# Token dispatch scaling on one core: first load cut into 16 and 112 partitions, weight loads moved behind it in the ScalarE queue

## The chip, the core and the metric

The kernel runs on one core of one Trainium2 chip. The metric is device time in microseconds (us), the median of several executions; lower is better.

## What is computed

```python
batch, seq, hidden, n_experts, k = 16, 1024, 512, 8, 2
# x: (16, 1024, 512) float32, expert_weights: (16, 1024, 2) float32
x_expanded = x[:, :, np.newaxis, :].repeat(k, axis=2)
out = x_expanded * expert_weights[..., np.newaxis]    # (16, 1024, 2, 512) float32
```

Every token, a row of 512 floats, is written out twice, each time multiplied by one of its two weights. The indices of the experts are not used. The kernel reads 33.6 MB of x and 0.13 MB of weights and writes 67.1 MB. There is one multiplication for each output element, so nearly all of the work is moving data.

## The kernel before

The 16384 tokens are dealt in eight groups of 2048. In a group each of the 128 partitions holds 16 consecutive tokens, that is 16 x 512 floats or 32 KB in one contiguous row (`rows`, lines 47 to 50).

Three pools hold the tiles. `w_tile` is one tile of 128 x 256 floats for all the weights. `x_pool` has two buffers of 32 KB per partition, each for one whole group. `o_pool` has four buffers of 32 KB per partition, and each of them takes the two products of eight tokens, half a group.

The work is issued from three engines:

- **SyncE queue.** First the eight weight loads (line 55), one for each group: 128 partitions x 32 floats, so 128 runs of 128 bytes, 16 KB in all. Then the sixteen stores (line 91), 4 MB each, one for each filled `o_tile`.
- **ScalarE queue.** The eight loads of x (line 70), 4 MB each: 128 partitions x 8192 floats. ScalarE computes nothing.
- **VectorE.** For every token and each of its two weights one `tensor_scalar` multiply (line 83) of 128 x 512 floats, 256 in all, 32 for each group and 16 for each store.

The order follows from the tile framework, which puts semaphore waits where a tile is written, read or used again. A load of x waits until VectorE is done with the group that lay in its buffer. A multiply that begins a new `o_tile` waits for the store that last used this buffer, four stores earlier. A store waits for its sixteen multiplies.

One more rule of order matters here. [...] In the kernel before, the first x load has semaphore 0 and the weight loads of groups 0 to 6 have 1 to 7 in the order of the program's text. The eighth weight load takes number 0 again, so it waits for the first x load. The second x load takes number 1 again, so it waits for the weight load of group 0. The later transfers wait for ones that ended long before, or for ones whose end they need anyway.

Of the kernel before, what the change touches and what calls it, by code (L numbers as in the profile page):

```python
# [1 line left out]

# [4 lines left out]


@with_exitstack
def kernel(  # L10
    ctx: ExitStack,
    tc: tile.TileContext,
    x: bass.AP,
    expert_indices: bass.AP,
    expert_weights: bass.AP,
    out: bass.AP,
):
    nc = tc.nc

    batch, seq, hidden = x.shape  # L20
    k = expert_weights.shape[-1]
    P = nc.NUM_PARTITIONS
    ntok = batch * seq
    assert ntok % P == 0
    A_TOTAL = ntok // P

    f32 = mybir.dt.float32
    row = k * hidden
    TX = 16
    TO = 8  # L30

    groups = [[[16]], [[16]], [[16]], [[16]], [[16]], [[16]], [[16]], [[16]]]
    assert sum(sum(sum(t) for t in g) for g in groups) == A_TOTAL

    xf = x.rearrange("b s h -> (b s) h")
    of = out.rearrange("b s k h -> (b s) (k h)")
    wf = expert_weights.rearrange("b s k -> (b s) k")

    w_pool = ctx.enter_context(tc.tile_pool(name="w_pool", bufs=1))
    x_pool = ctx.enter_context(tc.tile_pool(name="x_pool", bufs=2))
    o_pool = ctx.enter_context(tc.tile_pool(name="o_pool", bufs=4))

    w_tile = w_pool.tile([P, A_TOTAL * k], f32)

    def rows(of_all, done, T):
        return of_all[done * P : (done + T) * P, :].rearrange(
            "(p a) n -> p (a n)", a=T
        )  # L50

    done = 0
    for group in groups:
        T = sum(sum(t) for t in group)
        nc.sync.dma_start(
            out=w_tile[:, done * k : (done + T) * k], in_=rows(wf, done, T)
        )
        done += T

    done = 0  # L60
    for group in groups:
        T = sum(sum(t) for t in group)
        xr = rows(xf, done, T)
        outr = rows(of, done, T)
        a0 = 0
        for pieces in group:
            x_tile = x_pool.tile([P, TX * hidden], f32)
            at = 0
            for n in pieces:
                nc.scalar.dma_start(  # L70
                    out=x_tile[:, at * hidden : (at + n) * hidden],
                    in_=xr[:, (a0 + at) * hidden : (a0 + at + n) * hidden],
                )
                at += n
            ends = [sum(pieces[: i + 1]) for i in range(len(pieces))]
            first = 0
            for t in range(at):
                if t % TO == 0:
                    o_tile = o_pool.tile([P, TO * row], f32)
                for kk in range(k):  # L80
                    c = (done + a0 + t) * k + kk
                    o = t % TO * row + kk * hidden
                    nc.vector.tensor_scalar(  # L83
                        out=o_tile[:, o : o + hidden],
                        in0=x_tile[:, t * hidden : (t + 1) * hidden],
                        scalar1=w_tile[:, c : c + 1],
                        scalar2=None,
                        op0=mybir.AluOpType.mult,
                    )
                if t + 1 in ends or (t + 1) % TO == 0:  # L90
                    nc.sync.dma_start(
                        out=outr[:, (a0 + first) * row : (a0 + t + 1) * row],
                        in_=o_tile[:, first % TO * row : (t % TO + 1) * row],
                    )
                    first = t + 1
            a0 += at
        done += T


# [1 line left out]
_INS = ['x', 'expert_indices', 'expert_weights']  # L101
_OUTS = [((16, 1024, 2, 512), 'float32')]


# [23 lines left out]
```

## Time and profile before

| | |
|---|---|
| median of 3 runs | 240.84 us (240.41 to 241.1) |
| span of the profiled execution | 239.6 us |
| VectorE busy | 102.5 us (43%), 256 multiplies, mean 480 ns |
| bytes moved by DMA | 100.81 MB, mean 421 GB/s |
| share of 16 DMA engines: weights and stores (q1) | 65.3% |
| share of 16 DMA engines: loads of x (q10) | 33.0% |

The profile is that of one execution. Its times count from the start of the span. DVE is VectorE; ACTq and SPq are the instruction queues of ScalarE and SyncE, from which transfers are issued. The view of 40 slices gives for each slice of 6.0 us the busy share in tenths. The rows of DMA issues give the transfer, the queue, the count, the size of one transfer and the median time from issue to landing. A row of the chain of waits gives the start, the length and what was being waited for. A window row gives the stretch, its length, the busy time of the engines that work, the granted clock, the DMA busy share and the GB/s that were moved. Behind the views lie the trace's packet records: each transfer is cut into packets, and for each packet there are its start, its length, its queue and its size, but not the engine that moved it. A load of x is 128 packets of 32,768 bytes, a weight load 128 packets of 128 bytes.

### The profile page before, as it was taken

Reading aid. Unit: us, or ns where it says so; the run is one execution under the profiler, and the core shown is the slowest. Engines: PE = TensorE matmul, PEld = TensorE weight load, DVE = VectorE, ACT = ScalarE, POOL = GpSimd, SP = SyncE. Lnnn points to the kernel's source line nnn. Section 1 sums busy time; section 2 is a strip of 40 time slices with the busy share of each in tenths; the row PEclk is TensorE's granted clock in tenths of the full one; section 3 lists DMA queues with packets and bytes.
Section 4 is the critical chain, followed back from the end, with each engine's and each line's share of the span. In section 5 each row is a group of like instructions: output and inputs, shape, how many; then the busy total and the mean of one; then the engine's idle time right before and its main releaser. Section 6 shows DMA issues by size and latency. Waiting matters only on the chain.

```text
span 239.6 us, 369 instructions
## 1 busy us (share of the span) xinstructions
DVE 102.5 (43%) x256; POOL 0.2 (0%) x4
## 2 busy tenths in 40 slices
DVE  0089994067701905591064900739008485400000
POOL 0000000000000000000000000000000000000000
DMA  7999999999999999999999999999999999999994
GB/s 265 439 439 367 439 432 438 438 438 438 438 427 432 438 421 432 438 427 438 416 432 421 438 438 421 434 432 438 427 438 432 438 421 427 438 427 432 432 432 197
DMA packets 4610, 100.81 MB, mean 421 GB/s; under 512 B 1536, under 2 KB 1536, under 8 KB 1536
## 3 DMA queue, kind: packets, MB, share of 16 engines
q1 hardware_dynamic: 3456, 67.24, 65.3%
q10 hardware_dynamic: 1152, 33.55, 33.0%
q14 instruction: 2, 0.02, 0.0%
HBM read 33.69 MB, written 67.11 MB: 421 GB/s over the span
## 4 chain that ended last, share of the span: by engine, by line
DMA 62%; DVE 18%; another core or an unknown queue 5%; issue 0%; DVEq 0%
DMA out_dram<-o_tile 56%; DVE o_tile L83 18%; DMA x_tile<-in_x_dram 5%; DVEq L123 0%; DVEq L83 0%
## 5 line engine op out<-in xcount | busy, mean ns | idle before, releaser
L83 DVE TENSOR_SCALAR o_tile<-x_tile,w_tile 128x512 f32<-128x512 f32 x256 | 102.5, 480 | 104.1 <-DMA out_dram<-o_tile 76.4
L112 POOL MEMSET const-bfloat16-1.0<- 128x1 bf16 x1 | 0.1, 103 | 0.0
L112 POOL MEMSET const-uint8-127<- 128x1 uint8 x1 | 0.1, 103 | 0.0
L112 POOL MEMSET const-float32-1.0<- 128x1 f32 x1 | 0.1, 100 | 0.0
L112 POOL MEMSET const-float32-0.0<- 128x1 f32 x1 | 0.1, 99 | 0.2 <-issue 0.2
## 6 DMA issues: line engine op xcount, KB each, us to landing
out_dram<-o_tile SPq DMA_DIRECT2D x16, 4096.0 KB, 45.4
x_tile<-in_x_dram ACTq DMA_DIRECT2D x8, 4096.0 KB, 24.2
w_tile<-in_expert_weights_dram SPq DMA_DIRECT2D x8, 16.0 KB, 20.5
```

The costliest lines, as they stand in the source:

```text
L83: nc.vector.tensor_scalar(out=o_tile[:, o : o + hidden], in0=x_tile[:, t * hidden : (t + 1) * hidden], scalar1=w_tile[:, c : c + 1], scala ...
L112: nc = _bacc.Bacc("TRN2", target_bir_lowering=False, num_devices=1)
```

## The change

The first load of x becomes two loads, one of the partitions 0 to 15 and one of the partitions 16 to 127. All eight weight loads leave the SyncE queue and are issued on the ScalarE queue, right after these two. Then comes the second x load. It is meant to get the first bytes moving with a small transfer, and to keep the weights out of the way of the first load and of the first stores, which have the SyncE queue to themselves.

```diff
-    done = 0
     for group in groups:
-        T = sum(sum(t) for t in group)
-        nc.sync.dma_start(
-            out=w_tile[:, done * k : (done + T) * k], in_=rows(wf, done, T)
-        )
-        done += T
+        weights.append((sum(n for _, n in weights), sum(group)))
+    cuts = [0, 16, 128]
...
+    def load(i):
...
+        x_tile = x_pool.tile([P, TX * hidden], f32)
+        cols = rows(xf, done, T)[:, a0 * hidden : (a0 + n) * hidden]
+        for lo, hi in zip(cuts, cuts[1:]) if i == 0 else [(0, P)]:
+            nc.scalar.dma_start(out=x_tile[lo:hi, : n * hidden], in_=cols[lo:hi, :])
+        loaded.append(x_tile)
+        if i == 0:
+            for at, m in weights:
+                nc.scalar.dma_start(
+                    out=w_tile[:, at * k : (at + m) * k], in_=rows(wf, at, m)
+                )
+    for i in range(2):
+        load(i)
     for i, (done, T, a0, n) in enumerate(tiles):
+        x_tile = loaded[i]
...
-                nc.scalar.dma_start(
-                    out=x_tile[:, at * hidden : (at + n) * hidden],
-                    in_=xr[:, (a0 + at) * hidden : (a0 + at + n) * hidden],
-                )
...
+        load(i + 2)
```

The rest of the diff rewrites the loops and leaves the instructions alike: the same 256 multiplies in the same order on VectorE, the same sixteen stores on SyncE, and the same seven later loads of x. The ScalarE queue of the built program now has seventeen transfers where it had eight, and the semaphores fall differently. With their waits, the first of them are:

```
x_tile<-in_x_dram 16x8192                    semaphore 0
x_tile<-in_x_dram 112x8192                   semaphore 1
w_tile<-in_expert_weights_dram 128x32 x6     semaphores 2 to 7
w_tile<-in_expert_weights_dram 128x32        waits for semaphore 0
w_tile<-in_expert_weights_dram 128x32        waits for semaphore 1
x_tile<-in_x_dram 128x8192                   waits for semaphore 2
```

More of the change, by code (lines that the diff above doesn't have):

```diff
@@ L30 @@
     TO = 8
-    groups = [[[16]], [[16]], [[16]], [[16]], [[16]], [[16]], [[16]], [[16]]]
-    assert sum(sum(sum(t) for t in g) for g in groups) == A_TOTAL
+    groups = [[16], [16], [16], [16], [16], [16], [16], [16]]
+    assert sum(sum(g) for g in groups) == A_TOTAL
     xf = x.rearrange("b s h -> (b s) h")
@@ L50, in rows @@
         )
+    weights = []
+    for group in groups:
+        weights.append((sum(n for _, n in weights), sum(group)))
+    cuts = [0, 16, 128]
+    tiles = []
     done = 0
     for group in groups:
-        T = sum(sum(t) for t in group)
-        nc.sync.dma_start(
-            out=w_tile[:, done * k : (done + T) * k], in_=rows(wf, done, T)
-        )
-        done += T
-    done = 0
-    for group in groups:
-        T = sum(sum(t) for t in group)
-        xr = rows(xf, done, T)
-        outr = rows(of, done, T)
[L65 to L70, printed above, removed]
-                    out=x_tile[:, at * hidden : (at + n) * hidden],
-                    in_=xr[:, (a0 + at) * hidden : (a0 + at + n) * hidden],
-                )
[L74 to L88, printed above, removed]
-                    )
[L90 to L96, printed above, removed]
-        done += T
@@ new lines @@
+        T = sum(group)
+        a0 = 0
+        for n in group:
+            tiles.append((done, T, a0, n))
+            a0 += n
+        done += T
+    loaded = []
+    def load(i):
+        if i >= len(tiles):
+            return
+        done, T, a0, n = tiles[i]
+        x_tile = x_pool.tile([P, TX * hidden], f32)
[8 more added lines that the diff above has]
+                )
@@ new lines @@
+    for i in range(2):
+        load(i)
+    for i, (done, T, a0, n) in enumerate(tiles):
+        x_tile = loaded[i]
+        outr = rows(of, done, T)
+        for t in range(n):
+            if t % TO == 0:
+                o_tile = o_pool.tile([P, TO * row], f32)
+            for kk in range(k):
+                c = (done + a0 + t) * k + kk
+                o = t % TO * row + kk * hidden
+                nc.vector.tensor_scalar(
+                    out=o_tile[:, o : o + hidden],
+                    in0=x_tile[:, t * hidden : (t + 1) * hidden],
+                    scalar1=w_tile[:, c : c + 1],
+                    scalar2=None,
+                    op0=mybir.AluOpType.mult,
+                )
+            if (t + 1) % TO == 0:
+                nc.sync.dma_start(
+                    out=outr[:, (a0 + t + 1 - TO) * row : (a0 + t + 1) * row],
+                    in_=o_tile,
+                )
+        load(i + 2)
```

## Prediction, made before the run

> **What bounds the kernel now.** I read the slices first, then windows cut where the slices dip, then the chain of waits and the waits of the SyncE queue, and last the packet records. The page's slices:
>
> ```profile
> DVE  0089994067701905591064900739008485400000
> DMA  7999999999999999999999999999999999999994
> GB/s 265 439 439 367 439 432 438 438 438 438 438 427 432 438 421 432 438 427 438 416 432 421 438 438 421 434 432 438 427 438 432 438 421 427 438 427 432 432 432 197
> ```
>
> The DMA engines are full from the second slice to the last but one, VectorE is mostly waiting. Windows put numbers on the dips:
>
> ```profile
> 0.00:2.10 2.10, 0.00 (x0) 0.20 (x4) 1.00 0.48 128
> 2.10:4.20 2.10, 0.00 (x0) 0.00 (x0) 1.00 0.91 361
> 4.20:12.50 8.30, 0.00 (x0) 0.00 (x0) 1.00 0.97 416
> 12.50:21.00 8.50, 7.88 (x20) 0.00 (x0) 1.00 1.03 433
> 21.00:24.00 3.00, 3.00 (x9) 0.00 (x0) 1.00 0.89 293
> 24.00:146.00 122.00, 59.52 (x149) 0.00 (x0) 1.00 1.01 434
> 146.00:150.00 4.00, 0.00 (x0) 0.00 (x0) 1.00 0.97 377
> 150.00:236.00 86.00, 32.13 (x80) 0.00 (x0) 1.00 1.00 433
> ```
>
> At 434 GB/s the 100.81 MB take 232.3 us, so only 7.3 us of the 239.6 are not transfer at full rate: the start, a dip at 21 to 24 us, one at 146 us, the tail. The end moves by what the change adds to or takes from the time in which DMA engines stand idle or run slowly. The chain of waits begins with the part that the change touches:
>
> ```profile
> 0.73 12.37 DMA x_tile<-in_x_dram
> 13.09 0.03 issue
> 13.12 8.06 DVE o_tile L83 x21
> ```
>
> VectorE starts when the first load has landed at 13.09. The DMA engines go on without a break at that point, because the second load was issued long before:
>
> ```profile
> 8.24 0.33 ACTq L70 DMA_DIRECT2D x_tile<-in_x_dram  x1
> SPq L55 <- DMA x_tile<-in_x_dram: 8.6, 1, 8.6
> ```
>
> The first line (timeline) is the second x load: it had waited only for the weights of group 0, landed at 8.22. The second (waits of SyncE) is the eighth weight load, which waited for the whole first load. Nothing but stores stood behind it.
>
> The packet records give the unit of the sums. A packet of 32,768 bytes takes 1.213 us (27.0 GB/s; sixteen at once 432) and begins 1.218 us after the one before it. The engines begin their first packets at 1.85 to 2.85 us, mean 2.26, which is 1.53 after the issue at 0.73. The first packets end at 3.97 on average, 0.49 later than 1.213 us would. The first load's last packets end at 12.30 to 12.76, and its landing follows 0.33 later. The second load's packets follow at once; the first store's begin at 23.12 on average. Of the 1024 weight packets 720 run at 22 to 24 us: they alternate with x packets until these run out, then drain, in front of the first store. That is the dip at 21 us.
>
> [...] seven weight loads were issued by 4.4 us, and until the x packets ran out about one weight packet got through for each x packet. [...] The trace before has only 128-partition transfers. [...] no run here shows 16.
>
> **The change part by part.**
>
> *The second x load is issued later.* In the ScalarE queue it now stands behind the last weight load, which waits for the piece of 112 partitions. So nothing more is loaded until the whole first group has landed; call that time L. Queued behind the waiting weight load are all further x loads. The first store can't fill the hole: it needs sixteen multiplies, which begin at L and take 6.45 us (13.12 to the store's issue at 19.57). From L: one weight issue (0.33 to 0.38 us, the last one before took 0.33), then the x issue, then 1.53 us to the mean first packet: 1.9 us. If first packets again end 0.49 late: 2.4. Before, the second load's packets followed without a gap, so this is new idle time of all engines.
>
> *Weights leave the SyncE queue.* The 1024 packets now follow the first load in the same ring and drain in this hole, and the first store finds nothing before it. What that takes away is the dip: in before the first store's packets begin at 23.12 where sixteen x packets in a row end 16 x 1.218 after 2.75 (the first packets' end less one packet), at 22.24: 0.9 us gained. VectorE now also waits for the weights of group 0[...]. I cost it at nothing: while VectorE runs late, the second load keeps the engines busy for 9.7 us, and the first store comes 6.5 us after L.
>
> In one expression: before, the engines had moved 16 x packets each and began on the first store at 23.12, which is as if the second load had begun at 23.12 - 8 x 1.218 = 13.38. After, it begins at L + 1.9 to 2.4. The change is L + 1.9 (2.4) - 13.38. From there on both are full to the end with the same bytes: at L + 12.8 VectorE has freed the buffer for the third load and the second store is issued, while the second load and first store together keep the engines busy past L + 21.
>
> *The first load in two pieces.* If only the engines limit it, L is 13.1, or up to 0.4 less where sixteen descriptors and no weights in the way get the first packets started faster. Lower bound: L = 12.7. [...] With first packets at about 2.05 and the 0.33 of landing, L is 17.0 to 18.2. [...]
>
> *The loops.* Same multiplies and stores, same seven later loads: nothing.
>
> [...] 17.0 + 1.9 - 13.38 = 5.5 to 18.2 + 2.4 - 13.38 = 7.2, middle 6.4: 240.84 + 6.4 = 247.2 us.
>
> **The rivals.**
> - *Only the wait costs.* [...] L = 12.7 to 13.1, the change +1.2 to +2.1: about 242.4 us. For it: the engines' own rate is 27.0 GB/s, and the trace can't tell an engine's limit from a port's.
> - *Faster.* The start improves (0.5 late first packets, 0.4 of spread), the 0.9 us dip goes, and the new hole sets all engines off together, so the tail, where the last store's engines land between 236.4 and 238.8 us, shrinks by about 1 us; the dip at 146 us (57 GB/s short for 4 us, 0.5 us) may go too. The hole is 1.9: 1.9 - 0.9 - 0.9 - 1 - 0.5 = -1.4 with everything lucky, two thirds of it -0.9: about 239.9 us. Against it: the hole is certain from the waits, while tail and late dip have no tie to the first load.
> - *No change.* The same gains cancel the hole: 240.8.
> - *Worse dealing.* If the 112 partitions are dealt in rounds of sixteen neighbours, [...] about 271 us.
>
> **How the numbers follow.** Ports and wait 0.60 (247.2); wait alone 0.20 (242.4); faster 0.12 (239.9); no change 0.03 and worse dealing 0.05. Faster by over 0.3% (below 240.1): 0.12 with the lucky edge of the rest, 0.13. Within 0.3%: 0.07, which takes in the low edge of the wait alone. Slower: 0.80. The range runs from 241.6, leaving out the faster cases and the low edge of the wait alone, to 249.0, which takes in 248.0 and leaves the worse dealing out.
>
> **What would show it.** The second x load issued within 0.5 us after the first group's landing, and a window of about 2 us of almost no traffic there: the wait. [...] VectorE's start at 17 to 18.5 us: the ports; a start near 13 us refutes them. No dip where the first store begins: the weights. Full rate afterwards. I am wrong if the second load is issued before the first has landed, or if the tail's or the late dip's shape moves the end by more than the start does.

## The result, and the profile after

The changed kernel takes 254.0 us (median of 4 runs, 252.88 to 255.11) where the kernel before, run beside it, takes 240.68 us. The ratio is 1.055, with a 95% interval of 1.050 to 1.060. The direction was forecast, the size was not: 247.2 us with a range up to 249.0. The profiled execution of the changed kernel has a span of 251.1 us, 11.5 more than the 239.6 before; it is the fastest of its four runs, 1.1 us below their median, while the profiled execution before (241.35 us) lies 0.7 above its own. That is why the spans differ by 11.5 and the medians by 13.3. Where this text sums up a trace, it compares these two spans.

The 40 slices of the page after (6.3 us each):

```profile
DVE  0004969905463090459109090184503684700000
DMA  9995999999999999999999999999999999999994
GB/s 167 240 251 115 418 418 419 418 418 444 470 418 423 418 433 470 428 418 423 418 459 454 418 418 418 444 471 418 418 423 423 475 418 433 418 423 449 449 428 183
```

Nearly all of the loss is in the first four slices. DMA reads 9 in the first three of them, while the GB/s of the second and third, 240 and 251, are little more than half of the 439 that they were. This is the line to remember: the DMA engines are not idle, each packet takes longer, 3.58 us in the mean for the piece of 16 partitions and 1.8 to 2.7 in the seven steps of the piece of 112, where it was 1.213. Only the fourth slice, with a 5, shows idle engines. The slices after it count packets by their start, so 418 and 470 alternate; windows give the rate (stretch, length, busy time, clock, DMA share, GB/s; a share above 1 comes from packets that begin in a window and end after it):

```profile
1.70:5.50 3.80, 0.00 (x0) 0.00 (x0) 1.00 1.15 172
5.50:20.50 15.00, 0.00 (x0) 0.00 (x0) 1.00 0.97 237
20.50:23.60 3.10, 1.13 (x3) 0.00 (x0) 1.00 0.26 35
23.60:25.80 2.20, 2.20 (x7) 0.00 (x0) 1.00 1.18 373
25.80:30.00 4.20, 4.20 (x12) 0.00 (x0) 1.00 0.99 429
30.00:35.00 5.00, 5.00 (x14) 0.00 (x0) 1.00 1.01 374
35.00:132.00 97.00, 45.46 (x114) 0.00 (x0) 1.00 1.01 435
132.00:246.00 114.00, 44.60 (x112) 0.00 (x0) 1.00 1.00 432
```

The first line is mostly the piece of 16 partitions, the second the piece of 112, the third the hole, the sixth the dip where the first store begins. From 35 us on the rate is that of before. The chain of waits in order of time (start, length, what), from the piece of 112 partitions to the second x load:

```profile
1.13 21.04 DMA x_tile<-in_x_dram
22.16 0.02 issue
22.18 0.34 ACTq L80
22.52 0.04 issue
22.56 15.36 DMA x_tile<-in_x_dram
```

The piece of 112 partitions lands at 22.16, where the whole first load had landed at 13.09. The last weight load (L80) is issued 0.02 us later, and the second x load behind it at 22.56; before, that one went out at 8.24. So the load that began the chain before is followed here by a second one that could not overlap it. VectorE starts 0.3 us after the landing, when the first weights are there:

```profile
DVE o_tile L95 <- DMA w_tile<-in_expert_weights_dram: 22.5, 1, 22.5
```

The packet records of both traces give the account, in means over the sixteen engines (the records don't name them: sixteen packets run at a time, each beginning where one ends):

| | before, us | after, us | difference |
|---|---|---|---|
| end of the first load's last packets | 12.51 | 20.47 | +7.96 |
| from there to the second load's first packets | 0.02 | 3.36 | +3.34 |
| these first packets, beyond 1.213 | 0.00 | 0.70 | +0.70 |
| the last x packets before the first store, beyond 1.213 | 0.38 | 0.73 | +0.35 |
| from them to the store's first packets | 0.47 | 0.00 | -0.47 |
| sum | | | +11.9 |

The spans differ by 11.5. The first row is the split. The next two are the wait; about 0.8 us of the second comes in with the split, because the engines then end further apart (19.91 to 21.11 us, before 12.30 to 12.76) and the landing follows later (1.05 us after the last end, before 0.33); with the wait alone this row is 2.60. The last two are the dip where the first store begins: before, some 700 weight packets run there and leave a gap of 0.47 us; after, no weights are left (1020 of the 1024 packets begin at 19 to 23.6 us, mostly in the hole) and nothing stands before the store, but the x packets just ahead of it are lengthened more.

### The profile page after: what moved, and what is told of

It is laid out like the page before. It is cut to its first block, busy times and chain, and to the rows that moved or that the text cites. A ratio compares the mean times of both kernels' runs of the same rounds, so it can differ in the third digit from the quotient of the medians.

```text
span 251.1 us, 370 instructions
## 1 busy us (share of the span) xinstructions
DVE 102.6 (41%) x256; POOL 0.2 (0%) x4
## 4 chain that ended last, share of the span: by engine, by line
DMA 69%; DVE 12%; another core or an unknown queue 5%; ACTq 0%; DVEq 0%; issue 0%
DMA out_dram<-o_tile 54%; DMA x_tile<-in_x_dram 14%; DVE o_tile L95 12%; DVEq L132 0%; ACTq L76 0%; ACTq L80 0%; DVEq L95 0%
```

## The experiments

The first theory: two costs that add up, one of the split and one of the wait. Four kernels make a square: split or not, second load behind all weights or not. The changed kernel is the corner with both.

**The wait alone.**

```diff
-    cuts = [0, 16, 128]
+    cuts = [0, 128]
```

> The changed kernel with the first load whole again: all weight loads stay on the ScalarE queue ahead of the second x load. Theory (two costs that add up: the split makes the first load about 8 us longer, and the second load waits behind the last weight load): the first load lands at about 13 us, the second is issued right after, the engines stand idle for about 3.4 us and the first packets after that are 0.7 us late, so 240.7 + 4 = about 244.7 us. Rival (the split makes all of it, and the hole behind the first load is filled or made up later): 240.7 to 241.5 us. Rival (the wait makes most of it): 250 us or more.

Measured: 244.59 us, ratio 1.016 (1.009 to 1.022), span 243.3, as the theory had it; both rivals fall. Windows of this kernel:

```profile
1.70:12.50 10.80, 0.00 (x0) 0.00 (x0) 1.00 0.99 391
12.50:14.70 2.20, 1.16 (x3) 0.00 (x0) 1.00 0.34 49
14.70:16.60 1.90, 1.90 (x6) 0.00 (x0) 1.00 0.97 276
22.00:26.50 4.50, 4.29 (x11) 0.00 (x0) 1.00 0.94 350
```

The first load runs at its old speed and lands at 13.26; then there are 2.2 us with next to no traffic, and a slow start. The wait costs 3.7 of span by itself. The fourth line is the dip at the first store: it is there although all weights went through in the hole. By the packet records it is made of x packets lengthened by 0.81 us, with no gap behind them.

**The split alone.** The second load goes ahead of the other weights, so that it waits for nothing.

```diff
-        if i == 0:
-            for at, m in weights:
+        if i < 2:
+            for at, m in weights[:1] if i == 0 else weights[1:]:
```

> The changed kernel with the second x load moved ahead of the weight loads of groups 1 to 7, right behind the weights of group 0, so that it waits for nothing; the first load is still cut into 16 and 112 partitions. Theory of two costs: only the split remains, the first load's last packets end at about 20.5 us instead of 12.5, the second load's follow at once: 240.7 + 8 = about 248.7 us. Rival (the split costs only because it is followed by the wait): 242 us or less. Rival (weights draining in the first seconds of the store queue made the dip of the kernel before): about 0.9 us less than the theory, 247.8 us.

Measured: 249.2 us, ratio 1.035 (1.028 to 1.041), span 247.3. Its windows:

```profile
1.70:5.50 3.80, 0.00 (x0) 0.00 (x0) 1.00 1.32 198
5.50:20.50 15.00, 0.00 (x0) 0.00 (x0) 1.00 1.00 252
20.50:23.60 3.10, 0.89 (x3) 0.00 (x0) 1.00 0.91 361
```

The hole of 35 GB/s has become 361 GB/s, but the first load is as slow as in the changed kernel: its pieces land at 7.29 and 22.39. The split costs 7.7 of span. With the 3.7 of the wait that is 11.4, and the changed kernel has 11.5: the two costs add, and neither hides the other. The rival that the split costs only with the wait behind it falls. That the sum fits so closely is partly chance: the engines of the last store land over 3.2 us with the wait alone, over 1.4 with the split alone and over 2.1 with both. In medians the costs are 3.8 and 8.4, together 12.2, against 13.3. The rival about the weights is not tested here: they still drain before the first store, from the ScalarE queue, and the gap there is 0.49 us.

**Neither.** Both edits together. Only the weights' leaving the SyncE queue remains.

> Neither the split nor the wait: first load whole, weights of group 0 behind it, then the second x load, then the other weights, all on the ScalarE queue. What is left of the change is that the weights are off the SyncE queue. Theory of two costs: as before, 240.7 us, with a dip where the first store begins, since the changed kernel had the dip without weights in that queue. Rival (the weights draining ahead of the first store are the dip): 239.8 us, no dip.

Measured: 240.86 us against 240.78, ratio 0.9995 (0.997 to 1.002). Moving the weights to the ScalarE queue in this way is worth nothing that can be measured. The dip is there too:

```profile
20.00:24.00 4.00, 4.00 (x11) 0.00 (x0) 1.00 0.99 361
```

Here the weights still drain at that time, behind the second load, so this run doesn't settle what the dip is. The packet records of all five kernels say more. Where weights drain before the first store (the kernel before, the split alone, neither), 0.47 to 0.49 us pass between the last x packets and the store's first; where none are left (the wait alone, the changed kernel), nothing passes. So the gap goes with the weights. But in the two kernels without them the last x packets are lengthened by 0.73 and 0.81 us, against 0.00 to 0.38 in the others. The rival that the weights are the whole dip falls.

**Is it the cut, or which partitions?** Same bytes in both pieces, but the cut goes across the tokens of every partition (the free dimension).

```diff
-    cuts = [0, 16, 128]
+    cuts = [0, 2, 16]
...
-        for lo, hi in zip(cuts, cuts[1:]) if i == 0 else [(0, P)]:
-            nc.scalar.dma_start(out=x_tile[lo:hi, : n * hidden], in_=cols[lo:hi, :])
+        for lo, hi in zip(cuts, cuts[1:]) if i == 0 else [(0, n)]:
+            of_row = slice(lo * hidden, hi * hidden)
+            nc.scalar.dma_start(out=x_tile[:, of_row], in_=cols[:, of_row])
```

> As the run with the split and without the wait, but the first load is cut the other way: both pieces go to all 128 partitions, the first with two of each partition's sixteen tokens (512 KB, as the 16 partitions had), the second with the other fourteen. Theory (what costs is which partitions a piece reaches[...]): [...] nothing is lost: 240.8 us, first load landed at about 13 us. Rival (two transfers in the place of one cost, whatever their shape): 244 to 249 us.

Measured: 240.83 us, ratio 0.9994 (0.998 to 1.001). A first piece of 512 KB and a second of 3.5 MB, both to all partitions, cost nothing that can be measured; the second lands at 12.85. Its first load against that of the next run, in one window each, first this one:

```profile
1.70:12.50 10.80, 0.00 (x0) 0.00 (x0) 1.00 1.06 429
```

**Two equal halves.**

```diff
-    cuts = [0, 16, 128]
+    cuts = [0, 64, 128]
```

> As the run with the split and without the wait, but cut into the partitions 0 to 63 and 64 to 127. Theory of ports: [...] alone it took 10.7 us from first packet to last, and on one queue the second follows the first; so the first load lands at about 23 us and the time is about 240.8 + 10 = 251 us, more than with 16 and 112. Rival (a small first piece or an odd number of partitions per engine is the trouble; two equal halves overlap): 241 to 243 us.

Measured: 251.33 us, ratio 1.043 (1.041 to 1.045), and the same window of its trace:

```profile
1.70:12.50 10.80, 0.00 (x0) 0.00 (x0) 1.00 1.11 234
```

The pieces land at 13.56 and 23.57. Equal halves with even numbers of partitions are slower than 16 and 112 (two runs, 251.23 and 251.44, against 249.08 to 249.98). The rival with the small piece or the odd number falls.

**Loads alone.** To see the disputed cost by itself, loads follow one another, each waiting for the one before, and then two stores. This kernel and the two after it, which also hold loads alone, ran once each.

> Loads one at a time, each waiting for the one before, with other sets of partitions and other source rows; then two stores of 128 partitions, each alone. The multiplications and all but one sixteenth of the output are left out, so its time is only the sum of these transfers. What counts is each transfer's time from first packet to last. Theory A [...]: 16 neighbouring partitions take 3.6 us or more from any source rows, every eighth partition [...] about half, 2.4 us or less, from any source rows; 112 partitions take about 11 to 15 us, 0 to 31 and 0 to 63 [...] 4.9 and 9.7 us. Theory B (the source: 16 neighbouring rows of 32 KB are 512 KB of HBM in one piece): 16 neighbouring rows are slow into any partitions, every eighth row is fast, 1.2 us, into any partitions. Theory C (small loads are slow only as the first transfer of a kernel): all loads of 16 take 1.2 to 1.9 us, and 112 partitions about 8.5 us. A second store faster than the first by 0.5 us or more would say that the dip at the first store is a first use; equal says not.

Measured, in windows from each transfer's first packet to its landing. In order: 16 neighbours; all 128; 16 to 127; every eighth partition from sixteen neighbouring rows; 16 neighbours from every eighth row; every eighth from every eighth; 0 to 31; 0 to 63; 0 to 95; 0 to 111.

```profile
26.20:31.80 5.60, 0.00 (x0) 1.00 0.68 94
32.80:44.00 11.20, 0.00 (x0) 1.00 0.93 374
44.90:62.40 17.50, 0.00 (x0) 1.00 0.82 210
63.80:67.20 3.40, 0.00 (x0) 1.00 0.60 154
68.20:73.90 5.70, 0.00 (x0) 1.00 0.67 92
75.20:78.90 3.70, 0.00 (x0) 1.00 0.53 124
79.80:86.10 6.30, 0.00 (x0) 1.00 0.78 166
87.40:98.90 11.50, 0.00 (x0) 1.00 0.84 182
99.90:115.70 15.80, 0.00 (x0) 1.00 0.85 193
116.60:131.60 15.00, 0.00 (x0) 1.00 0.92 245
```

Sixteen neighbours take 5.6 us and every eighth partition 3.4; the source rows make little difference (5.7, 3.7). Theory B, the source, falls, and so does C: these loads are slow long after the start. That leaves A, the partitions written. Its sizes were met only in part. From first packet to last, as it counts, 16 neighbours took 4.4 us (3.6 or more expected), every eighth partition 2.6 and 2.8 (2.4 or less), 0 to 31 5.5 (4.9), 0 to 63 10.7 (9.7), and 16 to 127 took 16.9 (11 to 15): this last miss is the largest, and A doesn't explain it. All 128 partitions take less time than 16 to 127, 0 to 95 or even 0 to 63, with up to twice the bytes. The two stores alone take the same, 9.90 and 9.91 us of packets, each packet 1.22 us from the first on. So the dip is not the price of a first store by itself.

**How the 112 are dealt.**

> Loads alone again, the multiplications and all but one sixteenth of the output left out: seven loads of 16 partitions each, queued without waits between them, first such that the sixteen partitions of each lie seven apart (16, 23, 30, ... 121, then 17, 24, ...), then one load of the partitions 16 to 127, then seven loads of sixteen neighbours (16 to 31, 32 to 47, ...). Theory N (the 112 partitions are dealt to the engines seven neighbours each): the first seven loads move the same packets in the same order as the load of 112 and take as long, about 17 us from first packet to last, and the seven blocks of neighbours about 7 x 4.85 = 34 us. Theory R (dealt in rounds of sixteen neighbours): the blocks take as long as the load of 112. If the first seven take 11 us[...] and the load of 112 takes 17, then the dealing is another.

Measured, from first packet to landing: seven queued loads of sixteen partitions seven apart; the load of 112; seven blocks of sixteen neighbours.

```profile
14.20:30.60 16.40, 0.00 (x0) 1.00 0.87 224
44.00:60.60 16.60, 0.00 (x0) 1.00 0.86 221
73.80:107.00 33.20, 0.00 (x0) 1.00 0.95 111
```

The first two agree step by step. Mean lengths of the packets in each of the seven steps, us:

```
seven apart   2.00 2.11 1.68 2.10 2.04 2.23 2.02
load of 112   2.02 2.09 1.68 1.99 2.17 2.28 2.05
neighbours    3.59 4.63 4.63 4.63 4.63 4.63 4.63
```

The load of 112 runs as theory N says, like the loads seven apart, and in half the time of the blocks of neighbours. That each engine gets seven neighbours is inferred from these lengths, as the records don't name the engines. "Worse dealing" (theory R), to which the prediction gave 0.05, is not what happens. What the prediction had wrong is how long the packets then take, and the last run looks at that. The same load of 112 took 17.5 us in the run before and 16.6 here, so single runs of it differ by about 1 us.

**Sets of partitions apart.** The bursts go to eight sets of partitions, A to H; the table behind the result names them. Which engines of a set share a limit was assumed by the author, no run had shown it.

> Bursts of four queued loads each (the same partitions, four groups of rows), with a small load to all partitions between the bursts; the multiplications and all but one sixteenth of the output are left out. [...] Theory of fair sharing of ports alone: a packet takes 1.2 us in A, B and G, 2.4 for the sharing engines and 1.2 for the rest in C and D, 2.4 in E and H, 4.6 in F. Theory of coupling [...]: B, C and D about 2 us for all sixteen engines; A and G 1.2. [...] (any load that is not to all 128 partitions is slow): A and G 2 us or more.

Measured, in windows of the bursts C, D, G and H, from first packet to landing:

```profile
75.70:86.70 11.00, 0.00 (x0) 1.00 0.80 182
93.30:104.20 10.90, 0.00 (x0) 1.00 0.57 192
154.50:175.20 20.70, 0.00 (x0) 1.00 0.97 405
181.50:223.60 42.10, 0.00 (x0) 1.00 0.97 199
```

The table below is from the packet records and leaves out each engine's first packet of a burst, which has another length.

| burst, partitions | length of a packet, us |
|---|---|
| A, every fourth of 32 to 95 | mostly 1.213 |
| B, 11, 18, ... 116 | mostly 1.213 |
| C, 16, 23, ... 121 | 2.4 to 2.5 in all sixteen engines |
| D, 18, 25, ... 123 | 2.4 in two engines, 1.213 in most others |
| E, every eighth | 2.56 in all |
| F, 0 to 15 | 4.82 in all |
| G, 32 to 95 | 1.213 in all |
| H, 0 to 63 | 2.56 in all |

A, B, E, F, G and H are close to what was expected of fair sharing (1.2 in A, B and G, 2.4 in E and H, 4.6 in F), and D too. Against "any load that is not to all 128 partitions is slow", G moves 64 partitions at 405 GB/s, H at 199. Against coupling, which had B and D at about 2 us in all engines, B is fast (1.213) and so are most engines in D. C is the surprise: 1.2 was expected for all but a few engines, and all sixteen are slow. Why everyone is held back in this set, and not in D, is not settled: no other sets like these two were tried, and the source rows changed along with the partitions. What in the hardware makes the slow sets slow was not shown.

## Why the prediction was wrong in size

**"The second x load is issued later": right.** The prediction had 1.9 to 2.4 us from the landing L to the second load's packets, the late first ones counted. Measured: 23.84 - 22.16 + 0.70 = 2.38 us. The wait for the last weight load was read off the queue and the semaphores, and it fell where it was expected: the second load was issued 0.40 us after the landing. Without the wait the kernel takes 249.2 us, so 4.8 of the 254.0 are its share; alone it costs 3.8.

**"Ports and wait": right in kind.** That the first piece would be slow was the author's assumption: the trace before has loads to all 128 partitions only, at 1.213 us a packet. The runs show it: a burst of loads to the partitions 0 to 15 took 4.82 us per packet, 16 x 32,768 bytes in that time, so 109 GB/s. The lone piece in the changed kernel took less, 3.58 in the mean (1.92 to 5.50), and landed at 7.30. The case "only the wait costs" (242.4 us) falls with the split alone at 249.2; its price for the wait was too low as well, 244.6 in the run with the wait alone, of which 0.8 is the dip that it took to be gone. "Worse dealing" (271 us) falls with the run on dealing. That a port is the limit was not shown.

**"L is 17.0 to 18.2": this step failed.** With first packets at 2.05 and 0.33 of landing this left 15.8 us at most for the two pieces, an estimate of the author's for which no trace or run stood. In the changed kernel the first piece took 3.58, and the second from 5.50 to 20.47 us in the mean over the engines, 15.0, and 15.6 to its last packet: 19.2 together. The load of 112 alone shows what happened: in six of seven steps nearly all sixteen packets take about 2 us, where a packet to all 128 partitions takes 1.213. Burst C shows the same thing by itself: all engines at about 2.45 us. What holds them all back stays open. So the step is the term for the two pieces, mis-sized by 3.4 us or more. In addition the landing lags: from the last packet's end at 21.11 to the landing at 22.16 it is 1.05 us, where 0.33 was taken from a load to 128 partitions. Side by side, the prediction had 2.05 + 15.8 + 0.33 = 18.2 for L at most, and the trace has 1.92 + 3.58 + 15.6 + 1.05 = 22.16. VectorE started at 22.47 and not at 17 to 18.5.

**"What that takes away is the dip": wrong in the main.** The prediction gave the whole dip of 0.9 us to the weights. The gap in which they drain, 0.47 us, did go. But of the 0.85 us before, 0.38 were x packets that took longer, and without weights in the way this part grew to 0.73 in the changed kernel and 0.81 with the wait alone. The gain is 0.1 us and not 0.9. In those two kernels, and in the one before, the first lengthened packets begin 1.3 to 1.5 us after the issue of the first store; a store by itself begins without loss (1.22 us for its first packets). What lengthens them is open.

With the measured terms the prediction's own expression gives 22.16 + 2.38 - 13.38 = 11.2, and with 0.73 for the dip that stays 11.9; the spans differ by 11.5. The medians differ by 13.3 because of where the two profiled executions lie among the others. Why the three other runs of the changed kernel are 0.9 to 2.2 us longer than the profiled one stays open without a trace of them.

**The range** ended at 249.0 because the two cases with a slow first load lay at 248 and 271 with nothing between, both on the author's estimates. The measured 254.0 lies in that gap.

**Rivals.** "Faster" had the hole certain against it, and it was. Its hope for the start, first packets half a microsecond late, was not met: here the second load too, which begins on idle engines, has its first packets 0.70 late. The tail that it wanted shorter by 1 us stayed: the last store's engines land over 2.1 us where it was 2.4.

## What to carry to other kernels

Before a transfer is cut by partitions, time a load to the partitions of each piece: the cut into 16 and 112 cost 8.4 us here and that into halves 10.2, while a cut across the free dimension cost nothing measurable (240.83 us). A transfer put into a queue brings its waits with it: the weights were small, but the last of them waited for a whole load (until 22.16 us), and the next load stood behind it (22.56). And a DMA row full of nines says that engines are occupied; the GB/s beneath it, 240 and 251 here under nines that stood over 439 before, say how much they move.

## What the runs showed of the hardware

- Partitions 32 to 95 load at the rate of all 128 (1.213 us for each packet of 32,768 bytes, 405 GB/s), 0 to 63 at half of it (2.56 us, 199 GB/s), with the same number of partitions and a DMA share of 0.97 in both.
- In one set of sixteen partitions seven apart (16, 23, ... 121) all sixteen engines were slow (2.4 to 2.5 us a packet); in another (18, 25, ... 123) two engines were (2.4), most others not (1.213).
- In these runs a load to all 128 partitions that begins on idle engines has its first packets 0.5 to 0.8 us late, whether it is the first of the kernel (0.49 in the kernel before) or a later one (0.70 in the changed kernel); a store alone has not (1.22 us).
- The landing of a load to all 128 partitions followed its last packet by about 0.33 us. In the slow loads it was 0.4 to 1.2: 0.44 for 0 to 111, 0.57 for 16 to 127 and 1.17 for 0 to 15 in the loads alone, 1.05 for 16 to 127 in the changed kernel.
